# A new step order in the first stage of a hybrid decoder block, other weight shapes, and a longer fetch distance in the last product

## The chip, the cores and the metric

The kernel runs on one core of a Trainium2 chip. The metric is the device time of one execution in microseconds. The time before is the median of three runs. A profile is one more execution, taken by the hardware profiler. An execution takes a little longer than the span of its profile, since some of it lies outside the first and last instruction.

## The reference

One decoder block with batch 1, sequence 1024, width 1024, in float32. Two branches read the same normalised input; they are merged by gates, and a cross-attention to 256 memory tokens and a feed-forward layer (hidden width 2816) follow:

```python
u = rms_norm(h, norm_mix)
u_ssm, q, k, v, f_logit, gate_logits = split(u @ w_in)
y_ssm = gelu(s5_ssm(u_ssm, lam, dt, b, c, d_skip))      # diagonal state-space model, 32 groups of 16 channels
glu_a, glu_b = split(y_ssm @ w_glu);  out_a = glu_a * sigmoid(glu_b)
out_b = forgetting_attention(q, k, v, f_logit + b_forget) @ w_fox_o    # causal, 8 heads
gate_a, gate_b = split(sigmoid(gate_logits))
h = h + (gate_a * out_a + gate_b * out_b) @ w_mix_out
h = h + memory_cross_attention(rms_norm(h), rms_norm(mem, norm_mem_kv), w_mem_q, w_mem_kv, w_mem_o)
f_a, f_b = split(rms_norm(h) @ w_ffn_in)
h = h + (silu(f_a) * f_b) @ w_ffn_out
return rms_norm(h, norm_final)
```

## The kernel before

Every float32 operand of a product is split in two: a rounded part (a cast by ScalarE, `whi`, `uh`, `mh`, `oh`, line 173) and the rest (a subtraction by VectorE or GpSimd, `wlo`, `ul`, `ml`, `ol`, line 174). Each product is then three matmuls: high by high, low by high, high by low (lines 163 to 165). Loads and stores are issued by SP unless said otherwise; each engine takes its instructions in order, and a tile framework sets that order from the order of the program, with priorities and buffers of its own.

**Stage one (`stage_in`)** normalises the eight tiles of x and the two of the memory, transposes them, and computes the memory's keys and values and the input `u` of the state-space branch. Its order is written by hand in `ORDER_IN`, one letter a step:

- F fetches a tile into one of eight `xt` buffers, G a gain; Q takes the sum of squares (ACT, line 353), R the root (`rsqrt`, lines 188 to 198), S scales the tile (DVE line 212, or ACT and POOL lines 209 and 210 for "g").
- T transposes half a tile by four matmuls into a PSUM bank (line 218), E splits that bank into `uh` and `ul` (or `mh`, `ml`).
- D fetches a weight slot, W splits it ("g": with POOL). K and V are memory keys and values, k and v their results. U is the product for `u`, by 128 columns q and half h of the sequence; u copies it (line 421) and, at the second half, stores it in eight DMAs `u_d` (line 424).
- L loads and P computes, part by part, the coefficients of the state-space model; X issues idle matmuls.

In the order before, memory tiles and keys come first; x tiles follow between keys and values; U comes last. A key or U step loads all eight k-tiles of 128 columns (rows of 512 bytes) and does all of one output block.

**Stage two (`stage_ssm`)** computes the merge gates from `uT`: 32 units of 24 matmuls (16 column blocks by 2 halves, 5.45 us each at full clock), each with a sigmoid and a store `gate_d` issued by ACT (line 454). The state-space branch is put between them in four quarters q, by unit number:

```python
todo[4 + 7 * q] = [lambda q=q: s5.turn_weights(q)]
todo[5 + 7 * q] = [lambda q=q: s5.states(q, u_d)] + ([lambda q=q: s5.weights(q + 1)] if q < 3 else [])
todo[9 + 7 * q] = [lambda q=q: s5.out(q), lambda q=q: s5.store(q, y_d)]
```

`weights(q)` forms the quarter's weights on POOL and DVE (`fre`, `fim`, lines 1177 to 1180; `Gm`, 1188 to 1196), and its decay tables `EC` and `ES` by doubling (lines 1201 to 1211). `turn_weights` transposes them (lines 1226 and 1232, with the copy `F` on ACT, line 1227). `states` loads `xg` from `u_d` (line 1247), multiplies it by F (line 1254), and scans on DVE, which ends in `St` (lines 1259 to 1283). `out` multiplies St by Gm (line 1297), and `store` writes `yh` and `yl` in 16 DMAs to `y_d` (line 1307).

Attention, merge and cross-attention follow. **The feed-forward layer** is computed in sums and products of blocks that need 7 products where the plain way needs 8. Its first product writes the operands of the second, `c_d` and, from the weights, `t_d`, to memory. The second has 77 steps (`seq`: 7 products by 11 blocks) of 12 matmuls (`o_mm`, line 907). `o_get(m)` fetches the two halves of step m, 256 KB each (lines 890 and 896), and splits them. Steps 0 to 3 are fetched ahead of the last block's `gated`, and then, behind step m, step m + 4.

Of the kernel before, what the change touches and what calls it, by code (L numbers as in the profile page):

```python
# [19 lines left out]
P = 128  # L20
# [7 lines left out]
MH = 4  # L28
# [9 lines left out]
RSLOT_LATE = (0, 1, 2, 3, 4, 4, 5, 5, 6, 6, 7, 7)  # L38

ORDER_IN = """  # L40
G0 Fm Qm Fn D1 X24 Qn Rm D0 Sm F1 G1 Tm0 Rn Em0 Sn Tn0 F0 Tm1 W0 Q0 Tn1 En0 F2 Q1 W1g En1 Em1 K0 D2 F3 K1 R0
S0 T00 T01 k0 E00 Q2 W2g D3 E01 D4 S1 T10 Q3 W3 k1 D5 K3 K2 W4 E10 W5 D6 R1 k2 T11 k3 S2 F4 Q4 V0 F5 S3g T30
E11 D7 Q5 F7 T20 R2 T21 E21 E20 S4 E30 W6 W7 T40 V1 D8 S5 E40 W8 T31 V2 L0 T41 E31 V3 D9 Db T50 F6 Q6 v T51 W9
E51 U00 Da Q7 L1 E41 u00 R3 S6 Wa T60 E50 S7 T61 T70 Wbg E61 U10 E60 P0 U20 u10 T71 E70 E71 u20 P1 U21 U11 U30
P2 u30 U31 u11 u31 U01 u21 P3 P4 P5 u01
"""


# [17 lines left out]
def f32(ap):  # L66
    return ap.bitcast(F32)
# [50 lines left out]
class Block:  # L118
    BANKS = {"mm": 3, "sc": 2, "pv": 2, "misc": 1}

    def __init__(self, ctx, tc):
        self.tc, self.nc = tc, tc.nc
        nc = self.nc
        self.V, self.A, self.G, self.T, self.S = nc.vector, nc.scalar, nc.gpsimd, nc.tensor, nc.sync
        self.const = ctx.enter_context(tc.tile_pool(name="const", bufs=1))
        self.small = ctx.enter_context(tc.tile_pool(name="small", bufs=3))
        self.wpool = ctx.enter_context(tc.tile_pool(name="wpool", bufs=4))
        self.dram = ctx.enter_context(tc.tile_pool(name="dram", bufs=1, space=DRAM))
        self.psum = ctx.enter_context(tc.tile_pool(name="psum", bufs=2, space=PSUM))
        self.ident = self.const.tile([P, P], F32, name="ident")  # L130
        make_identity(nc, self.ident)
        self.mhalf = self.const.tile([P, 1], F32, name="mhalf")
        nc.vector.memset(self.mhalf, -0.5)
        self.junk = self.const.tile([P, 512], BF16, name="junk")
        self.nbank = 0
# [191 lines left out]
def stage_in(B, xp, s5, x, mem, g_mix, g_kv, w_in, w_mem_kv, uT, u_d, kv_d):  # L327

    V, A, T, S, small = B.V, B.A, B.T, B.S, B.small
    junk = xp.tile([P, D], BF16, name="junk")
    mT = Act(xp, "mT", 4, 8, ML, kg=4, name="m")
    tiles, gain, ss, rs, raw, w, ps, us, kv = {}, {}, {}, {}, {}, {}, {}, [], []
    names = {"m": -2, "n": -1, **{str(t): t for t in range(NT)}}

    def xtile(name="xt"):
        return xp.tile([P, D], F32, tag="xt", bufs=8, name=name)  # L340

    def fetch(t):
        tiles[t] = xtile()
        S.dma_start(tiles[t], mem[(t + 2) * P:(t + 3) * P, :] if t < 0 else x[t * P:(t + 1) * P, :])

    def gains(i):
        gain[i] = xtile("gain")
        S.dma_start(gain[i], (g_kv if i == 0 else g_mix).partition_broadcast(P))

    def square(t):  # L350
        if t % 2 == 0:
            ss[t // 2] = small.tile([P, 2], F32, name="ss2")
        A.activation(junk, tiles[t], AF.Square, scale=1.0 / 32, accum_out=ss[t // 2][:, t % 2:t % 2 + 1])

    def root(i):
        rs[i] = B.rsqrt(ss[-1][:, i % 2:i % 2 + 1] if i < 0 else ss[i], pool=i < 0)

    def scale(t, pool):
        i = t // 2
        r = rs[t][:, 0:1] if t < 0 else rs[i][:, t % 2:t % 2 + 1]  # L360
        B.norm_scale(tiles[t], tiles[t], r, gain[0 if t < 0 else 1], pool=pool)

    def turn(t, b):
        ps[t, b] = B.turn(tiles[t], b, ("misc", "pv")[b])

    def evac(t, b):
        B.turned(ps.pop((t, b)), b, *((mT, t + 2) if t < 0 else (uT, t)))

    def wget(i):
        if i < 4:  # L370
            src = w_mem_kv[:, i * P:(i + 1) * P]
        elif i < 8:
            src = w_mem_kv[2 * (i - 4) * P:2 * (i - 3) * P, 512:1024]
        else:
            src = w_in[:, C_U + (i - 8) * P:C_U + (i - 7) * P]
        raw[i] = B.wpool.tile([P, SLOT], F32, tag="raw", bufs=2, name="raw")[:, :D]
        S.dma_start(raw[i].rearrange("p (k c) -> p k c", k=D // src.shape[-1]),
                    src.rearrange("(k p) c -> p k c", p=P))

    def wsplit(i, pool):  # L380
        hl = [B.wpool.tile([P, WSLOT], F32R, tag=t_, name=t_)[:, :D] for t_ in ("whi", "wlo")]
        B.split(*hl, raw.pop(i), pool)
        w[i] = [t_.rearrange("p (k c) -> p k c", k=2 if 4 <= i < 8 else 8) for t_ in hl]

    def keys(h):
        ps["k", h] = B.bank("mm")
        B.gemm_t(ps["k", h][:, :ML], *w[h], mT, 0, 8)

    def keys_out(h):
        if not kv:  # L390
            kv.extend(xp.tile([P, D], F32R, tag="kv", bufs=4, name="kv") for _ in range(4))
        cs = slice(h * ML, (h + 1) * ML)
        B.split(kv[0][:, cs], kv[1][:, cs], ps.pop(("k", h))[:, :ML])
        if h == 3:
            for i in range(2):
                S.dma_start(kv_d[i], f32(kv[i]))

    def values(kk):
        wh, wl = w[4 + kk]
        for t in range(2):  # L400
            if kk == 0:
                ps["v", t] = B.bank("sc")
            for k in (2 * kk, 2 * kk + 1):
                B.mm3(ps["v", t], *mT.tok(k, t), wh[:, k % 2, :], wl[:, k % 2, :], k == 0, k == 7)

    def values_out():
        for t in range(2):
            cs = slice(t * 512, (t + 1) * 512)
            B.split(kv[2][:, cs], kv[3][:, cs], ps.pop(("v", t)))
        for i in range(2, 4):  # L410
            S.dma_start(kv_d[i], f32(kv[i]))

    def ssm_in(q, h):
        ps["u", q, h] = B.bank("mm")
        B.gemm_t(ps["u", q, h], *w[8 + q], uT, h, 8)

    def ssm_out(q, h):
        if h == 0:
            us.append(xp.tile([P, D], F32, tag="kv", bufs=4, name="us"))
        uv = us[q].rearrange("p (t c) -> p t c", t=8)  # L420
        A.copy(uv[:, :, 64 * h:64 * h + 64], ps.pop(("u", q, h)).rearrange("p (c t) -> p t c", t=8))
        if h == 1:
            for g in range(8):
                S.dma_start(u_d[8 * q + g].rearrange("t n c -> n t c"), uv[16 * g:16 * g + 16])

    prep = s5.prepare()

    acts = {"F": lambda a: fetch(names[a]), "G": lambda a: gains(int(a)), "Q": lambda a: square(names[a]),
            "R": lambda a: root(names[a]),
            "S": lambda a: scale(names[a[0]], a[1:] == "g"),  # L430
            "T": lambda a: turn(names[a[0]], int(a[1])), "E": lambda a: evac(names[a[0]], int(a[1])),
            "D": lambda a: wget(int(a, 16)), "W": lambda a: wsplit(int(a[0], 16), a[1:] == "g"),
            "K": lambda a: keys(int(a)), "k": lambda a: keys_out(int(a)), "V": lambda a: values(int(a)),
            "v": lambda a: values_out(), "U": lambda a: ssm_in(int(a[0]), int(a[1])),
            "u": lambda a: ssm_out(int(a[0]), int(a[1])), "L": lambda a: s5.load(int(a)),
            "P": lambda a: next(prep, None), "X": lambda a: B.warm(int(a))}
    for step in ORDER_IN.split():
        acts[step[0]](step[1:])


def stage_ssm(B, s5, qp, uT, w_in, gate_d, u_d, y_d):
# [29 lines left out]
def stage_tail(B, big, s2, sh, x, glu, aT, gate_d, kv_d, w_fox_o, w_mix_out, g_mq, w_mem_q, w_mem_o, g_ffn,  # L471
# [458 lines left out]
    for m in range(4):  # L930
        o_get(m)
    end(NF - 1)
    gated(NP - 1)
    out_sums(NP - 1, 1)
    gfin = B.bcast_gain(s2, g_fin)
    sets = [[B.bank(t_) for t_ in tags] for tags in (("sc", "sc", "misc", "mm"), ("mm", "mm", "pv", "pv"))]
    for m, (n, p) in enumerate(seq):
        if n == 3 and p >= NP - LAST:
            break
        for i in range(4):  # L940
            o_mm(m, i)
        if m + 4 < len(seq):
            o_get(m + 4)
        if n < 3 and p in (2, 4, 6, 8):
            t = 4 * (n - 1) + p // 2 - 1
            Hf[t] = slot(name="hf")
            S.dma_start(Hf[t], h_d[t])
        if p == NP - 1:
            for i in range(4):
                o_add(n, i)  # L950
                if n in (2, 5):
                    square(i if n == 2 else 4 + i, n // 3)
                if n == 4:
                    square(4 + i, 0)
                    finish(4 + i)
# [709 lines left out]
```

## Time and profile before

| what | before |
|---|---|
| median of three runs | 1619.08 us |
| lowest to highest | 1617.02 to 1619.61 us |
| profiled execution | 1622.52 us |
| its span | 1620.8 us |
| mean granted TensorE clock | 0.973 |
| TensorE busy | 1550.3 us (96%) |
| VectorE, ScalarE, GpSimd busy | 1018.0, 647.9, 255.9 us |

A busy time is the time in which an engine had an instruction under way; the share is that of the span. The granted clock is 1.0 where the chip's throttle lets TensorE run at full speed. A line such as "PE pv L218 <- DVE xt L212: 4.9, 2, 4.3" says that TensorE, at line 218, writing tile pv, waited for VectorE's write of tile xt at line 212, 4.9 us in all, twice, at longest 4.3 us. In a timeline, "[6.91 <-ACT oh L173]" is the idle time ahead of an instruction and what ended it. SPq and ACTq are the queues in which SP and ACT issue DMAs.

### The profile page before, as it was taken

To read this page: it belongs to the slowest core of one execution; us is meant where nothing else is said; L and a number is where in the kernel's file an instruction comes from. 1 tells how busy PE (TensorE), PEld (TensorE's weight loads), DVE (VectorE), ACT (ScalarE), POOL (GpSimd) and SP (SyncE) were. 2 spreads that over 40 slices of the span, in tenths; PEclk is the share of its full clock that TensorE was granted. 3 is DMA by queue.
4 is the path that set the end of the run, shared out by engine and by line. 5 is a ranking of instruction groups with operands and counts; after the bars stand their busy time and mean duration, and the time that the engine had idled before them with its cause. 6 is when DMAs were issued, how large, how long until landed. Compare 5 with 4: busy or idle time off the path is not lost.

```text
span 1620.8 us, 20540 instructions
## 1 busy us (share of the span) xinstructions
PE 1550.3 (96%) x7313; PEld 1274.2 (79%) x7313; DVE 1018.0 (63%) x1850; ACT 647.9 (40%) x1169; POOL 255.9 (16%) x339
## 2 busy tenths in 40 slices
PE   7799799998999999999999989999999999899997
PEld 6588688897777678888888767888888888688886
DVE  6645565434787776764455698777667776455555
ACT  6322333413566654222335565333333333244342
POOL 2025545100111213310002210001000000000001
PEclk7899899999999999999999999999999999899999
DMA  7746656633322543444202155445544445796642
GB/s 261 126 82 115 103 113 102 148 62 43 48 52 53 139 136 107 153 131 138 89 21 97 53 182 188 152 157 166 166 158 150 162 163 168 261 376 195 195 156 104
DMA packets 226102, 221.77 MB, mean 137 GB/s; under 512 B 50872, under 2 KB 159512, under 8 KB 226000
## 3 DMA queue, kind: packets, MB, share of 16 engines
q1 hardware_dynamic: 221392, 212.08, 46.8%
q10 hardware_dynamic: 4608, 8.39, 1.4%
q8 instruction: 57, 0.93, 0.2%
q14 instruction: 45, 0.37, 0.1%
HBM read 154.06 MB, written 64.32 MB: 135 GB/s over the span
## 4 chain that ended last, share of the span: by engine, by line
PE 79%; DVE 7%; DMA 6%; ACT 3%; POOL 2%; issue 2%; SPq 1%; DVEq 0%; POOLq 0%; ACTq 0%
PE mm L768 14%; PE pv L768 7%; PE mm L163 7%; PE mm L164 7%; PE mm L165 7%; PE mm L907 4%; PE sc L907 3%; PE sc L768 3%; PE sc L163 3%; PE sc L164 3%; PE sc L165 3%; PE pv L907 3%; DMA raw<-in_w_in_dram 2%; DMA xt<-in_x_dram 2%; PE misc L907 2%
## 5 line engine op out<-in xcount | busy, mean ns | idle before, releaser
L174 DVE TENSOR_TENSOR wlo<-raw,whi 128x1024 fp32r<-128x1024 f32 (+2 forms) x126 | 133.2, 1059 | 177.9 <-ACT whi L173 163.5
L173 ACT CAST whi<-raw 128x1024 fp32r<-128x1024 f32 (+2 forms) x129 | 116.0, 902 | 305.7 <-DMA raw<-in_w_in_dram 74.5
L163 PE MATMUL mm<-uh,whi 128*128 128x512 f32 x344 | 139.5, 406 | 0.3 <-DVE mc L1484 0.3
L164 PE MATMUL mm<-ul,whi 128*128 128x512 f32 x344 | 136.7, 397 | 0.0
L165 PE MATMUL mm<-uh,wlo 128*128 128x512 f32 x344 | 136.6, 397 | 0.0
L174 DVE TENSOR_TENSOR ol<-or,oh 128x1024 fp32r<-128x1024 f32 x73 | 88.7, 1224 | 73.3 <-ACT oh L173 71.4
L173 ACT CAST oh<-or 128x1024 fp32r<-128x1024 f32 x73 | 76.8, 1053 | 107.1 <-PE pv L907 41.8
L800 POOL TENSOR_TENSOR g<-a,c 128x512 f32<-128x512 f32 x22 | 35.3, 1607 | 389.9 <-ACT a L799 356.7
L165 PEld LDWEIGHTS mm<-uh,wlo 128*128 128x128 f32 x344 | 65.9, 191 | 13.6 <-DVE wlo L174 0.2
L163 PEld LDWEIGHTS mm<-uh,whi 128*128 128x128 f32 x344 | 66.5, 193 | 12.8 <-DVE mc L1484 0.6
L192 POOL TENSOR_TENSOR r<-ms,mhalf 128x1 f32<-128x1 f32 x26 | 17.5, 673 | 369.0 <-DVE ms L188 360.8
L164 PEld LDWEIGHTS mm<-ul,whi 128*128 128x128 f32 x344 | 66.1, 192 | 11.4
L1516 POOL TENSOR_TENSOR pl<-pf,ph 128x512 fp32r<-128x512 f32 (+1 forms) x32 | 36.9, 1153 | 239.2 <-DVE ph L1515 223.7
L1513 ACT ACTIVATE pf<-sc 128x512 f32<-128x512 f32 (+1 forms) x96 | 46.4, 490 | 52.5 <-DVE sc L1509 36.1
L768 PE MATMUL pv<-S3h,we 128*128 128x512 f32 x176 | 58.2, 390 | 1.3 <-ACT S3h L173 1.3
L907 PE MATMUL mm<-oh 128*128 128x512 f32 x106 | 41.5, 391 | 0.0
L907 PE MATMUL mm<-ol,oh 128*128 128x512 f32 x106 | 41.5, 391 | 0.0
L907 PE MATMUL mm<-oh,ol 128*128 128x512 f32 x106 | 41.4, 391 | 0.0
L163 PE MATMUL sc<-uh,whi 128*128 128x512 f32 x104 | 41.4, 398 | 0.0
L164 PE MATMUL sc<-ul,whi 128*128 128x512 f32 x104 | 41.0, 394 | 0.0
L165 PE MATMUL sc<-uh,wlo 128*128 128x512 f32 x104 | 40.9, 393 | 0.0
L1000 POOL TENSOR_TENSOR sg<-sg,ga 128x512 f32<-128x512 f32 x16 | 29.3, 1857 | 72.7 <-DVE sg L993 72.7
(574 smaller groups left out, 4566.3 us busy)
## 6 DMA issues: line engine op xcount, KB each, us to landing
or<-c_d SPq DMA_DIRECT2D x77, 256.0 KB
raw<-in_w_ffn_in_dram SPq DMA_DIRECT2D x22, 512.0 KB
rawb<-in_w_ffn_in_dram SPq DMA_DIRECT2D x22, 512.0 KB
wo<-in_w_ffn_out_dram SPq DMA_DIRECT2D x22, 512.0 KB
c_d<-g SPq DMA_DIRECT2D x44, 256.0 KB
t_d<-wo SPq DMA_DIRECT2D x44, 256.0 KB
or<-t_d SPq DMA_DIRECT2D x44, 256.0 KB
raw<-in_w_in_dram SPq DMA_DIRECT2D x20, 512.0 KB
```

Of the source, the lines that this page charges most:

```text
L163: T.matmul(ps, lh, rh, start=first, stop=False)
L164: T.matmul(ps, lh, rl, start=False, stop=False)
L165: T.matmul(ps, ll, rh, start=False, stop=last)
L173: self.A.copy(hi, src)
L174: (self.G if pool_lo else self.V).tensor_sub(lo, src, f32(hi))
L192: self.G.tensor_tensor(out=r, in0=v, in1=self.mhalf[:, 0:n], op=ALU.pow)
L768: T.matmul(ps, l_[:, k, :], r_, start=first and k == 0 and i == 0, stop=k == 3 and i == 2, skip_group_check=True)
L800: G.tensor_mul(g[:, 512:], a1, c1)
L907: T.matmul(ps, l_[:, gi], r_[:, 512:], start=n < 3 and p == 0 and k == 0 or n == 7 and p == 0 and k == 0, stop=p == NP - 1 and k == 2, ski ...
L1000: self.B.G.tensor_mul(self.out[j][:, cs], self.out[j][:, cs], ga)
L1513: A.activation(pf[:, off:], ps[:, off:], AF.Exp)
L1516: G.tensor_sub(pl[:, off:], pf[:, off:], f32(ph[:, off:]))
```

## The change

Six things are changed.

1. `ORDER_IN` is another order: all x tiles and the weights of U first, U by halves in the middle, memory tiles, keys and values last. The P steps are spread over the later part.
2. Each weight fetch (D) is now two k-tiles by 512 columns (rows of 2 KB); those of keys and values lie in `xt` buffers. K and U use them k-tile by k-tile: the new `outer` adds two k-tiles to four banks at a time (`mm`, `mm`, `mm`, `sc`). Keys are split out once for all heads.
3. `root` always uses the form with POOL's power instead of VectorE's Newton steps, as the memory tiles did.
4. The 32 stores `u_d` are issued by ACT instead of SP.
5. `out(q)` and `store(q)` stand one gate unit later.
6. In the second feed-forward product, `AHEAD` is 7: steps 4 to 6 are fetched ahead of the last `gated` too, and behind step m step m + 7.

Lines of the kernel after are higher by 9 to 11 behind `wget`: the U products are at line 388, the u_d stores at 433.

```diff
--- before.py
+++ after.py
@@ -38,11 +38,11 @@
 RSLOT_LATE = (0, 1, 2, 3, 4, 4, 5, 5, 6, 6, 7, 7)
 
 ORDER_IN = """
-G0 Fm Qm Fn D1 X24 Qn Rm D0 Sm F1 G1 Tm0 Rn Em0 Sn Tn0 F0 Tm1 W0 Q0 Tn1 En0 F2 Q1 W1g En1 Em1 K0 D2 F3 K1 R0
-S0 T00 T01 k0 E00 Q2 W2g D3 E01 D4 S1 T10 Q3 W3 k1 D5 K3 K2 W4 E10 W5 D6 R1 k2 T11 k3 S2 F4 Q4 V0 F5 S3g T30
-E11 D7 Q5 F7 T20 R2 T21 E21 E20 S4 E30 W6 W7 T40 V1 D8 S5 E40 W8 T31 V2 L0 T41 E31 V3 D9 Db T50 F6 Q6 v T51 W9
-E51 U00 Da Q7 L1 E41 u00 R3 S6 Wa T60 E50 S7 T61 T70 Wbg E61 U10 E60 P0 U20 u10 T71 E70 E71 u20 P1 U21 U11 U30
-P2 u30 U31 u11 u31 U01 u21 P3 P4 P5 u01
+F0 F1 G1 X24 F2 F3 D8 D9 F4 F5 F6 Q0 Q1 R0 S0 T00 E00 T01 E01 S1 T10 E10 T11 E11 W8 Q2 Q3 R1 S2 T20 E20 T21 E21 Da S3
+T30 E30 T31 E31 W9 F7 Db U00 Q4 Q5 R2 S4g T40 E40 T41 E41 Wag U10 S5 T50 E50 T51 E51 Wb U20 Fm Q6 Q7 R3 S6g T60 E60
+T61 E61 U30 u00 u10 u20 u30 S7 T70 E70 T71 E71 Fn G0 L0 U01 D0 D1 L1 U11 P0 D2 D3 Qm Qn Rm Rn U21 P1 Sm Tm0 Em0 Tm1
+Em1 U31 u01 u11 u21 u31 P2 Sn Tn0 En0 Tn1 En1 D4 D5 D6 D7 W0 P3 K0 W1 K1 P4 W2g K2 W3 K3 k P5 W4 V0 W5g V1 W6 V2 W7
+V3 v
 """
 
 
@@ -129,7 +129,7 @@
         self.psum = ctx.enter_context(tc.tile_pool(name="psum", bufs=2, space=PSUM))
         self.ident = self.const.tile([P, P], F32, name="ident")
         make_identity(nc, self.ident)
-        self.mhalf = self.const.tile([P, 1], F32, name="mhalf")
+        self.mhalf = self.const.tile([P, 2], F32, name="mhalf")
         nc.vector.memset(self.mhalf, -0.5)
         self.junk = self.const.tile([P, 512], BF16, name="junk")
         self.nbank = 0
@@ -353,7 +353,7 @@
         A.activation(junk, tiles[t], AF.Square, scale=1.0 / 32, accum_out=ss[t // 2][:, t % 2:t % 2 + 1])
 
     def root(i):
-        rs[i] = B.rsqrt(ss[-1][:, i % 2:i % 2 + 1] if i < 0 else ss[i], pool=i < 0)
+        rs[i] = B.rsqrt(ss[-1][:, i % 2:i % 2 + 1] if i < 0 else ss[i])
 
     def scale(t, pool):
         i = t // 2
@@ -367,33 +367,40 @@
         B.turned(ps.pop((t, b)), b, *((mT, t + 2) if t < 0 else (uT, t)))
 
     def wget(i):
-        if i < 4:
-            src = w_mem_kv[:, i * P:(i + 1) * P]
-        elif i < 8:
-            src = w_mem_kv[2 * (i - 4) * P:2 * (i - 3) * P, 512:1024]
-        else:
-            src = w_in[:, C_U + (i - 8) * P:C_U + (i - 7) * P]
-        raw[i] = B.wpool.tile([P, SLOT], F32, tag="raw", bufs=2, name="raw")[:, :D]
-        S.dma_start(raw[i].rearrange("p (k c) -> p k c", k=D // src.shape[-1]),
-                    src.rearrange("(k p) c -> p k c", p=P))
+
+        w_, c, kk = (w_mem_kv, 0, i) if i < 4 else (w_mem_kv, 512, i - 4) if i < 8 else (w_in, C_U, i - 8)
+        raw[i] = xtile("raw") if i < 8 else B.wpool.tile([P, SLOT], F32, tag="raw", bufs=2, name="raw")[:, :D]
+        S.dma_start(raw[i].rearrange("p (k c) -> p k c", k=2),
+                    w_[2 * kk * P:(2 * kk + 2) * P, c:c + 512].rearrange("(k p) c -> p k c", p=P))
 
     def wsplit(i, pool):
         hl = [B.wpool.tile([P, WSLOT], F32R, tag=t_, name=t_)[:, :D] for t_ in ("whi", "wlo")]
         B.split(*hl, raw.pop(i), pool)
-        w[i] = [t_.rearrange("p (k c) -> p k c", k=2 if 4 <= i < 8 else 8) for t_ in hl]
-
-    def keys(h):
-        ps["k", h] = B.bank("mm")
-        B.gemm_t(ps["k", h][:, :ML], *w[h], mT, 0, 8)
-
-    def keys_out(h):
-        if not kv:
-            kv.extend(xp.tile([P, D], F32R, tag="kv", bufs=4, name="kv") for _ in range(4))
-        cs = slice(h * ML, (h + 1) * ML)
-        B.split(kv[0][:, cs], kv[1][:, cs], ps.pop(("k", h))[:, :ML])
-        if h == 3:
-            for i in range(2):
-                S.dma_start(kv_d[i], f32(kv[i]))
+        w[i] = [t_.rearrange("p (k c) -> p k c", k=2) for t_ in hl]
+
+    def outer(pss, i, kk, rhs):
+
+        wh, wl = w[i]
+        for q, p_ in enumerate(pss):
+            for k in range(2):
+                rh, rl = rhs(2 * kk + k)
+                for n, (l_, r_) in enumerate(((wh, rh), (wh, rl), (wl, rh))):
+                    T.matmul(p_, l_[:, k, q * P:(q + 1) * P], r_, start=kk == 0 and k == 0 and n == 0,
+                             stop=kk == 3 and k == 1 and n == 2, skip_group_check=True)
+
+    def keys(kk):
+        if kk == 0:
+            for h in range(MH):
+                ps["k", h] = B.bank(("mm", "mm", "mm", "sc")[h])[:, :ML]
+        outer([ps["k", h] for h in range(MH)], kk, kk, lambda k: mT.rhs(k, 0))
+
+    def keys_out():
+        kv.extend(xp.tile([P, D], F32R, tag="kv", bufs=4, name="kv") for _ in range(4))
+        for h in range(MH):
+            cs = slice(h * ML, (h + 1) * ML)
+            B.split(kv[0][:, cs], kv[1][:, cs], ps.pop(("k", h)))
+        for i in range(2):
+            S.dma_start(kv_d[i], f32(kv[i]))
 
     def values(kk):
         wh, wl = w[4 + kk]
@@ -410,9 +417,11 @@
         for i in range(2, 4):
             S.dma_start(kv_d[i], f32(kv[i]))
 
-    def ssm_in(q, h):
-        ps["u", q, h] = B.bank("mm")
-        B.gemm_t(ps["u", q, h], *w[8 + q], uT, h, 8)
+    def ssm_in(kk, h):
+        if kk == 0:
+            for q in range(4):
+                ps["u", q, h] = B.bank(("mm", "mm", "mm", "sc")[q])
+        outer([ps["u", q, h] for q in range(4)], 8 + kk, kk, lambda k: uT.rhs(k, h))
 
     def ssm_out(q, h):
         if h == 0:
@@ -421,7 +430,7 @@
         A.copy(uv[:, :, 64 * h:64 * h + 64], ps.pop(("u", q, h)).rearrange("p (c t) -> p t c", t=8))
         if h == 1:
             for g in range(8):
-                S.dma_start(u_d[8 * q + g].rearrange("t n c -> n t c"), uv[16 * g:16 * g + 16])
+                A.dma_start(u_d[8 * q + g].rearrange("t n c -> n t c"), uv[16 * g:16 * g + 16])
 
     prep = s5.prepare()
 
@@ -430,7 +439,7 @@
             "S": lambda a: scale(names[a[0]], a[1:] == "g"),
             "T": lambda a: turn(names[a[0]], int(a[1])), "E": lambda a: evac(names[a[0]], int(a[1])),
             "D": lambda a: wget(int(a, 16)), "W": lambda a: wsplit(int(a[0], 16), a[1:] == "g"),
-            "K": lambda a: keys(int(a)), "k": lambda a: keys_out(int(a)), "V": lambda a: values(int(a)),
+            "K": lambda a: keys(int(a)), "k": lambda a: keys_out(), "V": lambda a: values(int(a)),
             "v": lambda a: values_out(), "U": lambda a: ssm_in(int(a[0]), int(a[1])),
             "u": lambda a: ssm_out(int(a[0]), int(a[1])), "L": lambda a: s5.load(int(a)),
             "P": lambda a: next(prep, None), "X": lambda a: B.warm(int(a))}
@@ -461,7 +470,7 @@
     for q in range(4):
         todo[4 + 7 * q] = [lambda q=q: s5.turn_weights(q)]
         todo[5 + 7 * q] = [lambda q=q: s5.states(q, u_d)] + ([lambda q=q: s5.weights(q + 1)] if q < 3 else [])
-        todo[9 + 7 * q] = [lambda q=q: s5.out(q), lambda q=q: s5.store(q, y_d)]
+        todo[10 + 7 * q] = [lambda q=q: s5.out(q), lambda q=q: s5.store(q, y_d)]
     for i, f in enumerate(gates):
         for g in todo.get(i, []):
             g()
@@ -878,7 +887,7 @@
             gated(j // 2 - 1)
 
 
-    LAST = 3
+    LAST, AHEAD = 3, 7
     ORDER = (1, 2, 6, 7, 5, 4, 3)
     seq = [(n, p) for n in ORDER for p in range(NP)]
     ops, Hf = {}, {}
@@ -930,6 +939,8 @@
     for m in range(4):
         o_get(m)
     end(NF - 1)
+    for m in range(4, AHEAD):
+        o_get(m)
     gated(NP - 1)
     out_sums(NP - 1, 1)
     gfin = B.bcast_gain(s2, g_fin)
@@ -939,8 +950,8 @@
             break
         for i in range(4):
             o_mm(m, i)
-        if m + 4 < len(seq):
-            o_get(m + 4)
+        if m + AHEAD < len(seq):
+            o_get(m + AHEAD)
         if n < 3 and p in (2, 4, 6, 8):
             t = 4 * (n - 1) + p // 2 - 1
             Hf[t] = slot(name="hf")
```

## The prediction

> **What bounds the kernel now.** I read the page first, then TensorE's waits over the whole span, the table of stages, and last the timelines around the long waits. The page (busy time and share of each engine; granted TensorE clock in 40 slices):
>
> ```profile
> span 1620.8 us, 20540 instructions
> PE 1550.3 (96%) x7313; PEld 1274.2 (79%) x7313; DVE 1018.0 (63%) x1850; ACT 647.9 (40%) x1169; POOL 255.9 (16%) x339
> PEclk7899899999999999999999999999999999899999
> ```
>
> TensorE is busy 96% of the span, so a gain must come from its few gaps and from the time that it runs below full clock. TensorE's waits (line waited for, total, times, longest; first group up to 170 us, then 170 to 420, then the one between 1390 and 1450):
>
> ```profile
> PE pv L218 <- DVE xt L212: 4.9, 2, 4.3
> PE misc L218 <- DVE xt L212: 4.7, 1, 4.7
> PE misc L218 <- DVE ul L174: 2.7, 1, 2.7
> ...
> PE pv L1297 <- DVE St L1283: 5.6, 2, 5.3
> PE pv L1254 <- ACT F L1227: 4.1, 1, 4.1
> ...
> PE sc L907 <- ACT oh L173: 6.9, 1, 6.9
> ```
>
> The first three belong to stage one, where x tiles come late; St and F to the first two quarters of the S5 branch; oh to the head of the second feed-forward product. All else is a solid stream. Stages (stretch; PE busy, PEld, DVE, ACT, POOL; clock; DMA share; GB/s):
>
> ```profile
> 0.00:20.00 20.00, 11.92 (x55) 9.29 (x56) 9.64 (x31) 11.01 (x18) 6.27 (x13) 0.70 0.79 274
> 80.00:100.00 20.00, 20.00 (x93) 16.52 (x93) 19.70 (x104) 5.48 (x11) 0.00 (x0) 1.00 0.46 78
> 160.00:180.00 20.00, 14.43 (x71) 12.49 (x70) 13.74 (x16) 8.41 (x12) 13.64 (x36) 0.83 0.54 74
> 200.00:220.00 20.00, 19.78 (x83) 16.89 (x84) 16.88 (x19) 6.36 (x14) 11.84 (x15) 0.85 0.66 135
> 1400.00:1420.00 20.00, 13.04 (x46) 9.78 (x45) 7.39 (x7) 7.33 (x7) 0.00 (x0) 0.74 1.03 362
> ```
>
> The clock is 1.00 where TensorE runs through (80 to 100) and 0.83, 0.85 and 0.74 in the stretches in and behind the long gaps. So a gap costs itself and a slow stretch behind it. How much, the timeline tells (start, duration, engine, line):
>
> ```profile
> 1399.03 0.39 PE L907 MATMUL sc<-whi 128*128 128x512 f32 x1
> 1401.52 0.39 PE L907 MATMUL mm<-whi,wlo 128*128 128x512 f32 x1
> 1408.82 1.22 PE L907 MATMUL sc<-oh 128*128 128x512 f32 x2 [6.91 <-ACT oh L173]
> 1414.51 0.39 PE L907 MATMUL sc<-oh 128*128 128x512 f32 x1
> ```
>
> Before the gap, twelve matmuls take one start each 0.226 us (1399.03 to 1401.52 are eleven steps). Behind it twelve take 1408.82 to 1414.51, 5.69 us, where 12 x 0.227 = 2.72 would do: 2.97 us lost, with the 6.91 of the gap 9.9 us. [...] The trace's 9.9 is used.
>
> **Part 1: the new order of stage one.** Before, x tiles alternate with memory keys and weights; the change loads all x first, does the four input products U (k-tile by k-tile into four banks) first, and keys and values last. The number of matmuls is the same: 438 units of 512 columns stand ahead of the first turn (L1226) in both orders, 96 of them gate work. So before, the gate work starts 96 x 0.227 = 21.8 us ahead of this row, at 112.0:
>
> ```profile
> 133.80 0.44 PE pv L1226 x4
> 6.41 1.06 ACT L353 ACTIVATE junk<-xt 128x1024 bf16<-128x1024 f32 x1 [4.33 <-DMA xt<-in_mem_dram]
> L353 ACT ACTIVATE junk<-xt 128x1024 bf16<-128x1024 f32 x10 | 10.6, 1057 | 11.6 <-DMA xt<-in_x_dram 6.8 <-DMA xt<-in_mem_dram 4.7
> L212 DVE SCALAR_TENSOR_TENSOR xt<-xt,r,gain 128x1024 f32<-128x1024 f32 x9 | 13.6, 1516 | 0.1
> L218 PE MATMUL misc<-ident,xt 128*128 128x128 f32 x40 | 8.1, 338 | 10.6 <-DVE xt L212 4.7 <-DVE ul L174 2.7 <-DVE ms L190 2.6
> L173 ACT CAST uh<-misc 128x256 fp32r<-128x256 f32 x16 | 5.9, 370 | 7.3 <-PE misc L218 5.4 <-DVE ul L174 1.8
> L174 DVE TENSOR_TENSOR ul<-misc,uh 128x256 fp32r<-128x256 f32 x16 | 6.7, 418 | 0.8 <-ACT uh L173 0.7
> ```
>
> After: the first tile lands at 6.4 as the memory tile does now, two squares (1.06 and a read of 0.19 each), the root on POOL (about 1.0 with what DVE does for it, an estimate) and the scale 1.28 bring the first scaled tile at about 11.3. Then each tile is two halves, each four transposes (mean 0.338), two casts (0.37) and a last subtraction (0.42): 1.35 + 0.74 + 0.42 = 2.5, through banks that are freed one after the other; four tiles 20 us. U00 starts at about 31.3. The bound below is DVE alone: four scales at 1.28 and sixteen subtractions at 0.42 with two weight splits at 1.2, 14 us, so 25; above, before's own waits for x, 4.9 + 4.7 more: 41. I take 31.3, since evacuation has one bank at a time. From there: U00 to U30, 96 x 0.227 = 21.8; 32 transposes of the later tiles at 0.13 (an estimate, below half of the mean 0.338, which holds cold and overlapping ones), 4.2; one cold stretch, 3.0; U01 to U31, 21.8. U31 ends at 82, and with the sixteen transposes of the memory tiles TensorE is through at 84.
>
> The root loses its Newton steps on DVE to one POOL operation, inside the 1.0 above. The S5 preparation (P), most of DVE's 19.70 busy us between 80 and 100, moves behind the first U products; DVE has little else from 60 on, so it ends about 90 by my count. It was needed when POOL began the gate weights, some 12 us ahead of the gate work, which would be 104 now: nothing waits, and each us above 104 costs at most one.
>
> Now the stores of u (u_d). They move from SP to ACT (L424 becomes an issue on ACT):
>
> ```profile
> L424 SPq DMA_DIRECT2D u_d<-us x32: 302/429/1158, 91.7 to 117.2; - x32
> L454 ACTq DMA_DIRECT2D gate_d<-gs x32: 326/326/361, 123.0 to 335.1; - x32
> L421 ACT COPY us<-mm 128x512 f32<-128x512 f32 x7 | 4.1, 581 | 10.1 <-PE mm L165 10.1
> L1041 SPq DMA_DIRECT2D craw<-in_c_re_dram x4: 767/1317/3131, 33.1 to 43.8; - x4
> ```
>
> On ACT's queue a copy (0.58) and eight issues per q stand ahead of the casts of the memory tiles; the new order has 24 of the 32 issues ahead of the cast that K0 needs. ACT can start when the first bank is done, 18 matmuls (4.1 us) before 82, at 78. Three copies and 24 issues take 3 x 0.58 + 24 x 0.43 = 12.1, the casts and the subtraction of the memory tile some 1.7 (two of 0.37, doubled in width, and 0.42): K0 starts at about 92, a gap of 8 us, and with it about 2.2 us of cold clock (what 160 to 180 lost, worked out below). Bounds per issue: 0.33 (gate_d on ACT now) and 1.317 (median of craw); I take 0.43, the same transfer on SP. Who waits: DVE's subtraction, TensorE's K and V, nothing on SP, which is through early. Keys are 96 matmuls of 256 columns (10.9), values 48 of 512 (10.9): gate work starts at 92 + 21.8 + 2.2 = 116, against 112. **Term: +4 us.** The 2 KB rows of the weights (before 512 B in keys and inputs) earn nothing in the sum: nothing waits for these weights in the new order, where D8, D9 run ahead; W8's load could be late by some us in the crowd of x (274 GB/s in the first 20 us), which lies inside the 25 to 41.
>
> **Part 2: the S5 branch behind it.** Start, duration, engine, line, idle before and releaser:
>
> ```profile
> 136.46 0.24 POOL L1180 COPY fre<-bb_re 128x64 f32<-128x64 f32 x1 [14.07 <-PE misc L1232]
> 170.32 0.68 DVE L1283 TENSOR_TENSOR St<-m,m 64x508 f32<-64x508 f32 x1
> 171.05 0.80 PE L1297 MATMUL pv<-St,Gm 128*128 128x128 f32 x2 [5.32 <-DVE St L1283]
> 192.26 1.05 ACT L173 CAST whi<-raw 128x1024 fp32r<-128x1024 f32 x1 [13.47 <-DMA raw<-in_w_in_dram]
> 188.64 0.57 SPq L1247 DMA_DIRECT2D xg<-u_d  x1
> 189.26 10.51 SPq L1307 DMA_DIRECT2D y_d<-yh  x8
> 199.87 5.31 SPq L1307 DMA_DIRECT2D y_d<-yl  x8
> ```
>
> St is late because POOL stood 14.07 us with the next quarter's fre (L1180), which waits for TensorE's L1232, ahead of this quarter's EC and ES. The new order of POOL has the EC chain first. And out(0), which needs St, comes one gate unit (24 x 0.227 = 5.45 us) later. St came 59 us behind the start of the gate work; with a start at 116 that is 175.4 even if POOL stood as now; out(0) needs it at 165.7 + 4 + 5.45 = 175.2. So either of the two removes the 5.32 us; I count it gone, with its cold stretch: 0.83 over 20 us is 6.8 us at half clock, some 4.4 of them in work, 2.2 lost. F at 200 is late because ACT waited 13.47 us for a weight whose slot DVE freed late, behind the same chain, and SP issued xg(1) at 188.64. With EC and ES some 10 us earlier (of the 14.07) xg(1) is issued near 180 and lands before 186, and F is needed at 116 + (200.2 - 112.0 - 5.32 - 2.2 - 4.11) = 192.6. 4.11 go, and 3.0 of cold clock (0.85 over 20 us is 6.0 at half). **Term: -5.3 - 2.2 - 4.1 - 3.0 = -14.6.** out(q) and store(q) later also shift y_d's sixteen issues (10.51 + 5.31 in this stretch) by 5.45; the next user behind them on SP is the turn's store, which the second quarter reaches with no gap now; cost nothing, and 4.1 if that cover is gone.
>
> **Part 3: seven steps ahead.** SP and ACT at the head of the second product:
>
> ```profile
> 1373.65 0.60 SPq L896 DMA_DIRECT2D or<-in_w_ffn_out_dram  x1
> 1400.84 0.64 SPq L890 DMA_DIRECT2D or<-c_d  x1
> 1407.73 1.04 ACT L173 CAST oh<-or 128x1024 fp32r<-128x1024 f32 x1 [13.72 <-DMA or<-in_w_ffn_out_dram]
> 1410.44 1.04 ACT L173 CAST oh<-or 128x1024 fp32r<-128x1024 f32 x1 [0.29 <-DMA or<-in_w_ffn_out_dram]
> ```
>
> Now SP issues the operands of steps 0 to 3 until 1373.65 and of step 4 only at 1400.84, behind all the stores of the last gated block; ACT gets it at 1407.73, and TensorE has eaten its four steps by 1401.9. After, steps 4 to 6 are issued ahead of those stores, with DMA half idle. They give TensorE 3 x 2.72 = 8.2 us of work, up to 1410.1. Step 7 then takes the place of step 4: issued at 1400.84, usable at 1408.82, 1.2 us in time; later steps arrive each 1.36 us (steps 4 to 6 reach ACT between 1407.73 and 1410.44) and are used each 2.72. What is late next: nothing, if that rate holds. ACT's three casts and DVE's three subtractions are only moved earlier, beside a full TensorE. **Term: -9.9.**
>
> **Sum.** +4 - 14.6 - 9.9 = -20.5. The profiled execution took 1622.52 (span 1620.8 and 1.7 outside it), 3.4 above the median 1619.08. It becomes 1602, and the median 1599 (1619.1 - 20.5 = 1598.6).
>
> **Rivals.** (1) *ACT blocked by its stores: slower.* One issue on ACT costs more than 20.5/24 + 0.43 = 1.28 us, and K0 waits for 24. For it: craw's issues on SP took up to 3.131 each. Against: gate_d's 0.326 on ACT. At 2.2, between craw's median and maximum, 24 x 1.77 = 42 us: 1641. Chance 0.12, with all else that ends above. (2) *F stays late*, since xg(1) or the weight ahead of it still waits: 7.1 back, 1606; chance 0.12. For it: the queue of y_d at 189.26 lies where it did. (3) *Fetching ahead only moves the gap* from step 4 to 7, DMA being at 1.03 of its share at 1400: 9.9 back, 1609; chance 0.10. Against: margin of 1.2 us and the idle slices before. [...] (5) It changes nothing that can be measured, by terms that cancel: 0.04.
>
> **How the numbers follow.** The forecast itself, 1590 to 1604, has 0.49. 0.2% (3.2 us) is about what a measurement of this kernel can tell from no change: faster means below 1615.9. Cases below that: 0.49 + 0.12 + 0.10 + 0.13 = 0.84. Lower end: U00 at 25 instead of 31 and issues of 0.33 (2.4): 1590; I go to 1588. Upper end: rivals 3 and 4 at 1609 and 1611 and, per issue, 0.99 (y_d's, 15.8 us for 16, 24 x 0.56 = 13.4): 1612; with a little of two at once 1614.
>
> **What would show it.** Right: first L388 matmul near 31; a TensorE wait for a cast of the memory tile of about 8 us near 84; gate work from 116; no wait for St above 1 us, none for F; no oh wait at 1400; PEclk full at 1400 to 1420. Wrong: ACT issues above 1 us; U matmuls at cold pitch beyond 45 us; a new wait at the third S5 quarter; oh late at step 7.

## The result: the same time within 0.2%, against a forecast of 1.2% faster

| | before | after |
|---|---|---|
| median of 22 runs each | 1619.55 us | 1623.08 us |
| lowest to highest | 1616.71 to 1624.03 | 1617.54 to 1627.40 |
| ratio, 95% interval | | 1.0019 [1.0010, 1.0028] |
| profiled execution, span | 1622.52, 1620.8 | 1620.26, 1618.5 |

By the medians the kernel after is 3.5 us slower, and the forecast was 1599. The profiled execution of after is one of the faster ones of its 22, and that of before is slower than all but two of its own 22, so between the two profiles the kernel after is 2.3 us shorter; the stages are therefore compared by their place in the span. The page of the profile after:

```profile
span 1618.5 us, 20538 instructions
PE 1549.4 (96%) x7313; PEld 1272.4 (79%) x7313; DVE 1012.6 (63%) x1821; ACT 649.8 (40%) x1170; POOL 259.7 (16%) x344
PEclk6989899999899999999999998999999999999999
```

TensorE's waits in the profile after, in the same three stretches as in the prediction (to 170 us, then to 420, and around the head of the second feed-forward product):

```profile
PE mm L388 <- ACT mh L173: 7.8, 1, 7.8
PE misc L218 <- DVE ul L174: 6.2, 1, 6.2
PE pv L218 <- DVE ul L174: 6.0, 2, 3.4
...
PE pv L1237 <- ACT m L1311: 3.8, 2, 2.9
PE pv L1308 <- DVE St L1294: 3.3, 2, 2.7
PE pv L1265 <- DMA xg<-u_d: 0.7, 1, 0.7
...
PE mm L777 <- ACT c L798: 1.3, 1, 1.3
```

The 6.9 us for oh at the end are gone, as forecast. The 7.8 us for the memory tile's cast are there, as forecast. But St still waits, and a wait that the prediction did not have stands beside it: the turn (L1237) for ACT's m (L1311), 3.8 us. The stages (us from the start of the span; first matmul of each, by its line):

| first matmul of | before | after | forecast |
|---|---|---|---|
| U00 (L388) | | 32.0 | 31.3 |
| K0 | | 93.7 | 92 |
| turn(0) (L1226, L1237) | 133.6 | 140.9 | 138 |
| states(1) (L1254, L1265) | 200.2 | 209.2 | 192.6 |
| attention (L1479, L1490) | 402.8 | 410.0 | |

Up to the first turn the kernel lost 7.3 us, where 4 were forecast. Up to attention it lost 7.2: the S5 branch, from which 14.6 us were to come, gave nothing here, and in a second profile, nearer the median, it lost 5 more (below). Behind attention the kernel is 9.5 us shorter (1208.5 against 1218.0), where the fetch distance lies. Table of stages of the profile after (columns as before):

```profile
20.00:40.00 20.00, 13.56 (x45) 10.40 (x46) 15.48 (x33) 10.92 (x22) 8.83 (x6) 0.54 0.60 163
40.00:60.00 20.00, 20.00 (x101) 16.54 (x99) 5.32 (x13) 6.79 (x17) 0.00 (x0) 1.00 0.70 173
80.00:100.00 20.00, 11.36 (x56) 10.10 (x55) 15.49 (x58) 5.67 (x9) 1.32 (x1) 0.74 0.67 130
180.00:200.00 20.00, 15.34 (x76) 13.65 (x77) 11.16 (x21) 8.64 (x12) 9.80 (x31) 0.80 0.53 89
200.00:220.00 20.00, 19.31 (x83) 15.86 (x84) 10.57 (x12) 6.34 (x14) 14.16 (x14) 0.86 0.75 167
1410.00:1430.00 20.00, 20.00 (x90) 16.56 (x89) 10.33 (x11) 8.43 (x8) 0.00 (x0) 1.00 1.00 368
```

The clock is 0.80 and 0.86 between 180 and 220, much as it was 0.83 in 160 to 180 and 0.85 in 200 to 220 before; it is 1.00 at the head of the second feed-forward product, where it was 0.74.

### The profile page after: what moved, and what is told of

It reads as the page before. It is cut to its first block, busy times and chain, and to the rows that moved or that the text cites. A ratio compares the mean times of both kernels' runs of the same rounds, so it can differ in the third digit from the quotient of the medians.

```text
span 1618.5 us, 20538 instructions
## 1 busy us (share of the span) xinstructions
PE 1549.4 (96%) x7313; PEld 1272.4 (79%) x7313; DVE 1012.6 (63%) x1821; ACT 649.8 (40%) x1170; POOL 259.7 (16%) x344
## 4 chain that ended last, share of the span: by engine, by line
PE 79%; DVE 7%; DMA 6%; ACT 3%; issue 2%; POOL 2%; ACTq 1%; SPq 0%; POOLq 0%; DVEq 0%
PE mm L777 14%; PE pv L777 7%; PE mm L163 6%; PE mm L164 6%; PE mm L165 6%; PE mm L916 4%; PE sc L916 3%; DMA raw<-in_w_in_dram 3%; PE sc L777 3%; PE sc L163 3%; PE sc L165 3%; PE sc L164 3%; PE pv L916 3%; PE mm L388 3%; PE misc L916 2%
## 5 line engine op out<-in xcount | busy, mean ns | idle before, releaser
L163 PE MATMUL mm<-uh,whi 128*128 128x512 f32 x280 | 113.8, 407 | 0.3 <-DVE mc L1495 0.3
L164 PE MATMUL mm<-ul,whi 128*128 128x512 f32 x280 | 112.2, 401 | 0.0
L165 PE MATMUL mm<-uh,wlo 128*128 128x512 f32 x280 | 111.6, 399 | 0.0
L192 POOL TENSOR_TENSOR r<-ms,mhalf 128x1 f32<-128x1 f32 (+1 forms) x30 | 20.2, 676 | 368.7 <-DVE ms L188 350.6
L165 PEld LDWEIGHTS mm<-uh,wlo 128*128 128x128 f32 x280 | 54.1, 193 | 11.1 <-DVE wlo L174 0.2
L163 PEld LDWEIGHTS mm<-uh,whi 128*128 128x128 f32 x280 | 54.2, 193 | 10.6 <-DVE mc L1495 0.6
L164 PEld LDWEIGHTS mm<-ul,whi 128*128 128x128 f32 x280 | 54.1, 193 | 9.2
L163 PE MATMUL mm<-yh,whi 128*128 128x512 f32 x104 | 40.7, 392 | 0.0
L165 PE MATMUL mm<-yh,wlo 128*128 128x512 f32 x104 | 40.6, 390 | 0.0
```

The lines of the kernel that those rows point to most:

```text
L163: T.matmul(ps, lh, rh, start=first, stop=False)
L164: T.matmul(ps, lh, rl, start=False, stop=False)
L165: T.matmul(ps, ll, rh, start=False, stop=last)
```

## The experiments

All kernels were compared with runs of before on the same chip; "against before" is the ratio with its 95% interval. The medians of before in the three groups were 1620.2, 1619.3 and 1620.7, so a difference between two kernels of different groups carries some 1 us of that.

**The fetch distance alone.** The kernel before with:

```diff
-    LAST = 3
+    LAST, AHEAD = 3, 7
...
+    for m in range(4, AHEAD):
+        o_get(m)
...
-            o_get(m + 4)
+            o_get(m + AHEAD)
```

> The kernel before with only the fetch distance of the second feed-forward product raised from 4 to 7. Theory of the prediction: the 6.9 us wait at the head of that product and its half-clock stretch go, -9.9 us: 1609 to 1611, ratio near 0.994. What the profile after already hints: 1.3 us of it come back as a wait inside the last block of the first product, so -8.6. Rival (the gap only moves from step 4 to step 7, or its gain is lost in the loads that it collides with): 1619, ratio 1.000.

1611.2 us, 0.9950 [0.9934, 0.9966]. The only wait of TensorE between 1370 and 1440 is

```profile
PE mm L768 <- ACT c L789: 0.7, 1, 0.7
```

So the theory holds: 9.0 us (5.5 to 10.7 by the interval), of the 9.9 forecast. The 0.7 (1.3 in the kernel after) are a new wait in the last block of the first product, probably since ACT's casts of steps 4 to 6 now lie there; that was not tried.

**The stores of u on SP again, in the kernel after.**

```diff
-                A.dma_start(u_d[8 * q + g]...
+                S.dma_start(u_d[8 * q + g]...
```

> The kernel after with the 32 stores of u issued by SP again. Theory: the 7.8 us wait of K0 for the cast of the memory tile is made by the 24 issues ahead of it on ACT's queue; without them TensorE goes from U to K with a gap below 2 us, the gate work starts near 111 instead of 119, and the time falls by 6 to 8 us against the kernel after. Rival: the cast would be as late without them, since the memory tiles are normalised late: the wait stays above 5 us and the time changes by less than 2.

1612.9 us, 0.9945 [0.9923, 0.9967], 10.1 below the kernel after, where 6 to 8 were expected. The wait for the memory tile falls from 7.8 to 3.0 us, and it is now DVE's subtraction that comes last (both profiles, the row of u_d and the waits from 80 to 100 us and from 140 to 340):

```profile
L433 ACTq DMA_DIRECT2D u_d<-us x32: 309/442/467, 80.6 to 96.5; - x32
```

```profile
PE mm L388 <- DVE ml L174: 3.0, 1, 3.0
PE pv L1265 <- DMA xg<-u_d: 4.9, 1, 4.9
PE pv L1237 <- ACT m L1311: 2.3, 2, 1.4
```

The price of an issue on ACT was taken rightly: a median of 0.442 us, against 0.43. The first turn is back at 133.5, and St is no longer waited for. In its place stand xg at the second quarter (4.9 us) and the turns for m (2.3): the forecast's second rival.

**The quarter's output back at unit 9, in the kernel after.**

```diff
-        todo[10 + 7 * q] = [lambda q=q: s5.out(q), lambda q=q: s5.store(q, y_d)]
+        todo[9 + 7 * q] = [lambda q=q: s5.out(q), lambda q=q: s5.store(q, y_d)]
```

> The kernel after with out and store of each quarter at gate unit 9 + 7q as before. Theory: St is ready at a fixed time (about 180 in the profile after), so out(0) waits a whole unit more: its wait rises from 2.7 to about 8 us, and the time by 4 to 6 us; the later quarters show no wait in either. Rival: the place of out matters on ACT and SP (its table loads and its 16 stores queue behind gate work), and the earlier place gives time back: no change or faster by some us.

1617.8 us, 0.9985 [0.9975, 0.9994], 5.3 below the kernel after. The theory's wait came, and the time fell all the same (waits from 140 to 340 us):

```profile
PE pv L1308 <- DVE St L1294: 9.0, 2, 8.8
PE pv L1265 <- ACT F L1238: 2.7, 1, 2.7
```

A longer wait for St (9.0 against 3.3) and a faster kernel: by the time the rival holds, and the later place costs 5.3 us. The waits do not show why. That of the turn for m (3.8) is gone, but the two above add up to 11.7 us, against 7.8 in the profile after. Attention begins at 410.3, as in that profile (410.0), which shows one of the shorter executions; in the second profile of the kernel after, further down, it begins at 415.0. So what the later place costs with u on ACT is seen in the times and not traced to one wait.

**Each gate store one unit later, in the kernel after.** `gate` keeps its store and issues the one before it:

```diff
-        gs = qp.tile([P, 512], F32, tag="gs", bufs=2, name="gs")
+        gs = qp.tile([P, 512], F32, tag="gs", bufs=3, name="gs")
         A.activation(gs, ps, AF.Sigmoid)
-        A.dma_start(gate_d[j * P:(j + 1) * P, 512 * h:512 * h + 512], gs)
+        held.append((gate_d[j * P:(j + 1) * P, 512 * h:512 * h + 512], gs))
+        if len(held) > 1:
+            A.dma_start(*held.pop(0))
...
```

It rests on these rows of ACT, SP and DVE in the kernel after (start, duration, engine, line, idle before and releaser):

```profile
149.25 0.60 ACT L462 ACTIVATE gs<-mm 128x512 f32<-128x512 f32 x1 [5.84 <-PE mm L165]
167.57 0.34 ACTq L463 DMA_DIRECT2D gate_d<-gs  x1
167.95 0.74 ACT L1270 COPY zre<-pv 64x256 f32<-64x256 f32 x2 [18.10 <-DMA raw<-in_w_in_dram]
...
154.12 0.37 SPq L149 DMA_DIRECT2D raw<-in_w_in_dram  x1
...
170.26 0.69 DVE L1273 TENSOR_TENSOR m<-zre,EC 128x512 f32<-128x512 f32 x1 [7.08 <-ACT zre L1270]
```

The sigmoid at 149.25 was followed by nothing for 17.7 us; then came the store, and behind it the copies zre, though TensorE had begun the states at 149.0. DVE, free for 7.08 us, began the scan at 170.26; so 7 us of the hold reached the scan. What ended the 18.10 us of ACT's idle time ahead of the copies was, by the row of zre, a load of a gate weight (`raw`), which neither the store nor the copies read; the last one issued until then is SP's at 154.12. In the kernel before, the store at the same place came 0.35 us behind the end of its sigmoid (142.93 against 142.58). With u on SP it came 1.6 us behind (144.10 against 142.48), and the row of zre names a transfer of `Tt`. Why this store waits for that load no run shows.

> The kernel after with each gate store issued one gate unit later, behind the next sigmoid (three buffers instead of two). [...] With the store later the copies come at about 153, St before 170, the wait for St (2.7) goes, and with it the half clock behind it and the wait of the next turn (2.9): -5 to -9 us against the kernel after. Rival: St is late because POOL and DVE form EC and ES late (the chain ends at 153 in either kernel), so the copies are early and the scan is as late as now: no change.

1618.4 us, 0.9993 [0.9984, 1.0002], 4.7 below the kernel after, where 5 to 9 were expected. The wait for St is gone altogether; the turn's for m grows:

```profile
PE pv L1240 <- ACT m L1314: 7.5, 2, 5.3
```

So the hold of ACT made St late, but with out at unit 10 most of the gain turns into a new wait. The clean test is the same edit with out at unit 9:

> The kernel after with out at unit 9 + 7q and each gate store one unit later; u stays on ACT. Against the kernel with out at 9 alone (1617.8, wait for St 8.8). Theory: the gate store that waits for the weight load's landing made St late, so with the same place of out the wait for St falls from 8.8 to below 2 and the time by 7 to 11 us, to 1607 to 1611. Rival: St is late by the later start of the gate weights on POOL (113 instead of 100) and the wait stays above 5: 1615 to 1618.

1611.7 us, 0.9951 [0.9938, 0.9964], 6.1 below the kernel with out at 9 alone. ACT and TensorE there:

```profile
150.21 0.33 ACTq L465 DMA_DIRECT2D gate_d<-gs  x1
150.58 0.74 ACT L1273 COPY zre<-pv 64x256 f32<-64x256 f32 x2 [0.40 <-PE pv L1268]
PE pv L1311 <- DVE St L1297: 3.8, 2, 3.1
```

The copies begin at 150.58 instead of 167.64, and the wait for St falls from 9.0 to 3.8 us. It was expected below 2. The rest lies on DVE, ahead of the scan:

```profile
158.77 1.39 DVE L1208 TENSOR_TENSOR Gm<-w,w 64x512 f32<-64x512 f32 x2 [3.77 <-POOL w L1203]
162.51 1.39 DVE L1210 SCALAR_TENSOR_TENSOR Gm<-w,w 64x512 f32<-64x512 f32 x2 [2.35 <-POOL w L1203]
163.93 0.69 DVE L1276 TENSOR_TENSOR m<-zre,EC 128x512 f32<-128x512 f32 x1
```

DVE waits 6.1 us for POOL ahead of the next quarter's Gm, and the scan behind it begins at 163.93. So POOL, on which the rival laid it, has a share; no run takes it away alone.

**The output one unit later, alone, in the kernel before.**

```diff
-        todo[9 + 7 * q] = ...
+        todo[10 + 7 * q] = ...
```

> The kernel before with out and store one unit later, nothing else. By the prediction's step the wait for St (5.3 us) goes, and with it 2.2 us of half clock: 1612 to 1614. Theory now: only one gate unit is left between out and the next quarter's turn, which writes the banks that out's results still fill until ACT has read them, and the stores of y run beside xg: a new wait of 1 to 5 us at the turn and the wait at the second quarter's states stays or grows: 1616 to 1622.

1628.1 us, 1.0047 [1.0035, 1.0059]: slower by 7.4 us, where the prediction's step gave 7 us of gain, and beyond what was expected by then. The rows of ACT and TensorE:

```profile
192.66 1.04 ACT L173 CAST whi<-raw 128x1024 fp32r<-128x1024 f32 x1 [19.33 <-DMA raw<-in_w_in_dram]
195.93 1.09 ACT L1300 ACTIVATE m<-pv 128x512 f32<-128x512 f32 x2
196.67 1.09 PE L1226 MATMUL pv<-ident,fre 128*128 128x128 f32 x4 [15.06 <-ACT m L1300]
PE pv L1226 <- ACT m L1300: 15.9, 2, 15.1
PE pv L1297 <- DVE St L1283: 0.8, 1, 0.8
```

The wait for St did fall, from 5.6 to 0.8. But one unit later on ACT, reading out's results (m, L1300) stands behind the cast of a gate weight that waited 19.33 us for its load. The next quarter's turn writes the banks `pv` that m still holds, so TensorE stood 15.06 us. In the kernel before, at unit 9, m is read at 175, ahead of that cast, which comes at 192.26 there:

```profile
175.06 0.60 ACT L1300 ACTIVATE m<-pv 128x512 f32<-128x512 f32 x1 [0.79 <-PE pv L1297]
```

**Two edits undone together: u on SP, out at unit 9.** This is the kernel after with the first two of the diffs above.

> The kernel after with the stores of u on SP and out and store of each quarter at unit 9 + 7q: of the change, the order of stage one, the weight shapes, POOL's root and the fetch distance are left. Theory: the 16 stores of y (y_d) are issued ahead of the next quarter's load xg again and no longer beside it, so the wait for xg at the second quarter (4.95 us with u on SP and out at unit 10) shrinks, while St is ready at 171 and out(0) now needs it at about 165: its wait of 5 us comes back. The two cancel: 1605 to 1613, the median near that of u on SP with out at unit 10 (1612.9), but with a smaller spread. Rival: the later place only costs (as with the kernel after, where the earlier place was 5 us faster): 1605 to 1607.

1604.8 us, 0.9912 [0.9897, 0.9928], just below both ranges and nearest to the rival's; the wait of 5 us for St that the theory asked for does not come back. St is in time here (0.2 us): the copies zre begin at 147.45 instead of 167.64 (the kernel with u on ACT and out at 9), and the scan at 155.04 instead of 169.94, though POOL begins its S5 weights at 111.6, hardly earlier than there (112.5):

```profile
PE pv L1265 <- ACT F L1238: 3.3, 1, 3.3
PE pv L1308 <- DVE St L1294: 0.2, 1, 0.2
```

**The same, and the gate store later, with out at 10 and at 9.**

> The kernel after with the stores of u on SP and each gate store one unit later. Theory: with u on SP the gate store ahead of the state copies held ACT only from 142.5 to 144.1, so the later store gains nothing at St; the wait for xg at the second quarter is what is left. Time within 2 us of the kernel with u on SP alone (1612.9). Rival: the holds of ACT by gate stores also cost at later quarters: 1605 to 1608.

1611.6 us, 0.9955 [0.9938, 0.9973]: within 2 us of the kernel without it, as the theory said.

> The best kernel so far (u on SP, out at 9, 1604.8) with each gate store one unit later. Theory: its state copies were held by a gate store for only some 2 us and St is in time, so nothing is gained there; F at the second quarter (3.3 us) waits for a weight and not for a gate store: 1603 to 1607. Rival: the gate store also holds F: 1599 to 1602.

1601.6 us, 0.9886 [0.9873, 0.9898]: 3.2 below, inside the rival's range, with the wait for F at 2.5 us instead of 3.3; the intervals of the two kernels just touch. It is the fastest kernel of this study, 19.1 us below its before.

**Stage one alone.** The kernel before with the new order, the weight shapes and POOL's root only (u on SP, out at 9, fetch distance 4).

> The kernel before with only the new order of stage one, the new weight shapes and POOL's root: u on SP, out at 9, fetch distance 4. Theory: what is left of the best kernel without the fetch distance, so 1604.8 + 9 = 1612 to 1615, 5 to 7 us below before. Rival (the two parts overlap, stage one's gain is partly noise of the attention stage): 1617 to 1620.

1614.0 us, 0.9952 [0.9938, 0.9966]: 6.6 us, as the theory said. With the fetch distance's 9.0 it makes 15.6, and the two together (u on SP, out at 9) were measured at 14.6 below their before. Where the 6.6 us come from, the first turn and the start of attention tell (first start of each line):

```profile
L1237 PE MATMUL pv<-ident,fre x16: 270/272/273, 136.7 to 281.2; 128*128 128x128 f32 x16
L1490 PE MATMUL mm<-hb x48: 220/395/582, 396.1 to 553.1; 68*128 68x512 f32 x24, 68*128 68x128 f32 x8, 68*128 68x256 f32 x8, 68*128 68x384 f32 x8
```

The first turn comes 3.1 us later than in the kernel before (133.6), attention 6.7 earlier (402.8). So stage one itself gets no shorter by its new order; the S5 branch behind it does, by 9.8 us, with St in time (0.2 us) and 3.2 us of wait for F.

**Second profiles.** The times of the kernel with u on SP and out at 10 lay in two groups.

> A second profile of the kernel after with the stores of u on SP, whose times lie in two groups, 1604 to 1607 and 1613 to 1616. Theory: what differs is the wait for xg at the second quarter (4.95 us in the first profile) and the half clock behind it, and the length of the attention stage by half-clock stretches. Rival: stage one differs (tiles landing later).

Profiled again it took 1611.5 instead of 1604.3. Up to attention the same waits stand in both (3.0 us for K0, 4.9 and 4.2 for xg); what differs is the clock (first profile, then second):

```profile
80.00:100.00 20.00, 15.95 (x117) 14.50 (x117) 17.10 (x60) 8.43 (x13) 3.52 (x2) 1.00 0.66 130
1380.00:1400.00 20.00, 20.00 (x90) 16.57 (x89) 8.45 (x12) 2.25 (x3) 1.73 (x1) 1.00 0.73 255
```

```profile
80.00:100.00 20.00, 15.91 (x97) 14.51 (x96) 15.93 (x59) 6.56 (x10) 2.50 (x2) 0.83 0.66 128
1380.00:1400.00 20.00, 17.70 (x71) 14.16 (x70) 10.07 (x14) 4.05 (x5) 1.73 (x1) 0.91 0.59 193
```

In one execution the 3.0 us wait of K0 was followed by full clock, in the other by 0.83 over 20 us. Neither the theory's place nor the rival's was the only one: the first turn came at 133.5 and 135.8, attention at 396.8 and 400.6, and the rest of the difference, 3.4 us, lies behind, where the clock was 1.00 and 0.91 and a wait for ACT's c took 0.9 and 2.3 us.

> A second profile of the kernel after, whose times lie between 1617.5 and 1627.4 while its profiled execution took 1620.3. Theory: attention starts at 410 again (+7 against before), and a longer execution is longer behind that, in half-clock stretches of the attention stage. Rival: the S5 quarters differ, with a longer wait for xg or F at the second one, so that attention starts at 413 or later.

It took 1623.7, like the median. Attention began at 415.0 instead of 410.0, so the rival is right on the place, but not on the cause: the first turn came at 140.9 in both, xg took 0.7 us in both and F none. The turn's wait for m was 5.2 us in all instead of 3.8 and St's 3.5 instead of 3.3; the rest was half clock (0.93 and 0.90 in 280 to 300 and 300 to 320, where it was 1.00).

The three edits in one table (medians; all with the new stage one and distance 7):

| | out at 9 | out at 10 |
|---|---|---|
| u on SP | 1604.8 | 1612.9 |
| u on ACT | 1617.8 | 1623.1 (the change) |
| u on SP, gate store later | 1601.6 | 1611.6 |
| u on ACT, gate store later | 1611.7 | 1618.4 |

## Why the prediction was wrong

**Part 1, stage one: the mechanism right, the size off.** The walk gave U00 at 31.3 and K0 at 92; they came at 32.0 and 93.7, with the forecast gap of 8 us (7.8). The term was +4 and was 7.3 in the profile: K0 was 1.7 late, and the half clock behind the gap was taken as 2.2 us, while the clock of 0.74 over 80 to 100 is 10.4 us at half, some 6 of them after K0's start at 93.7 (0.50 from 94 to 98, 0.79 from 98 to 102), which is 3 us lost. What the prediction did not ask is whether the part is worth having without the stores on ACT: the new order alone gains 6.6, and the stores alone take back 10 to 13 us.

**Part 2, the S5 branch: the step that failed.** It was -14.6 and came to about 0 in the first profile and to +5 in the second. In the first, TensorE's waits there fell only from 9.7 us (St and F) to 7.8 (the turn, St and xg), and the half clock that was to go stayed. Its step on POOL was right: ES was done at 152.9 (158.7 before), though the S5 weights began 13 us later (113.5 against 100.1).

```profile
158.22 0.43 DVE L1211 TENSOR_TENSOR ES<-d,d 128x256 f32<-128x256 f32 x1
152.53 0.42 DVE L1222 TENSOR_TENSOR ES<-d,d 128x256 f32<-128x256 f32 x1
```

With nothing but the new order, weight shapes and root, the S5 branch is 9.8 us shorter ("Stage one alone"), so this half of the term held. Two other sentences fell. "Either of the two removes the 5.32 us; I count it gone" looked at POOL and DVE alone, and left out ACT between states and scan: a store held the copies for 17.7 us, and a load of a weight ended that wait. And "cost nothing, and 4.1 if that cover is gone" for the later output looked at SP's queue and not at ACT's, where m moved behind a weight's cast, nor at the banks that the turn shares with out: alone, this edit costs 7.4 us. (A small slip beside it changes nothing: 59 us behind 116 is 175.1, not 175.4.)

**Part 3, the fetch distance: right.** -9.9 forecast, -9.0 measured alone.

**The sum.** The new order -6.6 and the distance -9.0 make -15.6 (-14.6 when measured together). From there the stores of u on ACT take back 13.0 at the old place of out (1617.8 - 1604.8), and the later place 5.3 more (1623.1 - 1617.8): that sums to +3 or +4, and the change was measured at +3.5 by its own 22 runs. These steps lie on one path, so that they add up is no proof of them beyond the 15.6 against 14.6. The forecast's rival 1 named the stores on ACT as the mechanism on the slow side, but priced them by the time of an issue; each issue cost what was assumed (0.442 us against 0.43). With u on ACT and out at 9, 6.1 us go with the gate store moved (1617.8 to 1611.7); the same edit gives 3.2 with u on SP, where the store held ACT only some 2 us, so the long hold by itself is worth some 3 to 6 us. With the gate store later in both, u on ACT still costs 10.1 (1611.7 against 1601.6). About half of that is stage one's later end (the first turn at 141.2 against 135.9), 2.9 more lie between there and attention (401.9 against 393.7), and the rest behind. Rival 2 (xg or F late) did come where the other waits were gone: 2.5 to 4.9 us of wait, where it counted 4.1 and 3.0 of cold clock behind it. Rival 3 did not come: step 7 was in time. The 12 us of half clock in U that make the 1611 of rival 4 in the upper end of the range are an estimate that no run bears out: U began at half clock (0.50 in 32 to 36 us, 0.72 in 36 to 40), some 3 us, and ran at 1.00 from 40 on.

What stays open: why a gate store waits for the load of a weight, through which wait the later place of out costs 5.3 us with u on ACT, why the half clock follows a wait of 3.0 us in one execution and not in another, and how much of the kernel's spread of 10 us is that. No experiment changed the clock by itself.

## What to carry to other kernels

Before an instruction is moved on an in-order engine, list what it will stand behind there, and what that waits for: a cast that waits 19 us for a load cost TensorE 15 us as soon as a bank's reader was moved behind it. When transfers are moved between issuing queues, look in the trace at what ended the idle time around each issue: here a gate store came 17.7 us behind its sigmoid, and what ended the wait was a load that has nothing to do with it. Several edits in one change hide each other: of this one, two parts gained 15 us and two lost 18, and only taking them apart showed it.

## What the runs showed that was not expected

- One gate store, whose issue takes 0.34 us, held ACT for 17.7 us; by the row of zre a load of a weight ended the wait.
- The same wait was not equally dear: behind K0's 3.0 us the clock was 1.00 in one execution and 0.83 over 20 us in another, and by the first turn the two executions were 2.3 us apart, of 7.2 in all.
- How much of the fetch distance's gain is half clock could not be told: its 9.0 us, 5.5 to 10.7 by the interval, fit the whole 9.9 us of the trace before, and the 6.91 us of the gap without the 2.97 behind it as well.
